# An encoder layer in 3-way split float32 on one core: gating two token tiles from SBUF, the prompt's weight remainders on VectorE, and three pairs of copies exchanged

## The chip, the core and the metric

The kernel runs on one core of a Trainium2 chip. Its engines are TensorE (PE in the profile, with PEld for its weight loads), VectorE (DVE), ScalarE (ACT), GpSimd (POOL) and SyncE (SP), which here issues nearly all DMAs. The metric is device time in microseconds (us). The kernel before takes 946.03 us, the median of three runs (943.36 to 946.63).

## The reference

One encoder layer is applied, with the same weights, to a prompt of 256 tokens and a sample of 2048 tokens of width 1024. What must be computed, cut to what matters here:

```python
h = rms_norm(x, g_pre)
q, k, v, z_a, u_f, z_f = split(h @ w_in)            # six parts of 512 columns
y_a = neighbourhood_attention(q, k, v, rpb)         # 64-column grid, 8x16 windows, 8 heads
y_f = fft2(u_f over tokens and 64 channels).real @ w_fourier + b_fourier
mixed = concat(rms_norm(y_a, g_na) * silu(z_a), rms_norm(y_f, g_f) * silu(z_f))
out = x + rms_norm(mixed @ w_out, g_post)
```

All is float32. The factors g_na and g_f are folded into the weights of `w_out`, and the inverse norm of a token is applied after that product, so the product's input from the Fourier half is `y_f * silu(z_f)`: this is the gating that the change moves.

## The kernel before

A float32 product is made of three matmuls: each operand is split into a rounded high part (a cast to float32r) and the remainder (operand minus high part), and `mm3` (L171) adds high·high, low·high and high·low. So before each product one engine casts (most often ACT) and one subtracts (most often DVE).

The program runs in stages. TensorE's order is written out throughout. In the first stages, up to `man.close()` at L961, the order of the other engines is written out too: they run in the order of the code. After that a scheduler orders ACT, DVE, POOL and SP, until the last quarter of the Fourier output (L1342), from where the order is the code's again.

- **Projections v and u of the first six token tiles** (L601 to L742). `x_split(c)` casts tile c (L293, ACT) and takes its remainder (L296, DVE). `diag` (L327, ACT) spreads the tokens' inverse norms over ten 128x128 diagonals, `dg`, which `spread` (L321) transposes on TensorE into PSUM. `r_sum` (L467, DVE) and `r_put` make sums of weights and store them.
- **The prompt's other four projections** (L745 to L783): sixteen steps b, each with 24 matmuls of 256 columns. `b_raw(b + 2)` casts the weights of step b + 2 (L578, ACT) and takes the remainder `wl` (L579), on GpSimd for the four weights in `WP` and on VectorE for the others. Between them VectorE scales and sums the sample's input for the next stage (L417, L440, L446), and `op_split` (L495) prepares that stage's first weights.
- **The sample's projections** (L785 to L959), Fourier stages (L961 to L1073).
- **Fourier output** (L1310 to L1365): four blocks e of 128 channels. `y_mm` makes three pieces ti of a block on TensorE, `y_out` adds the bias (L1264, ACT) and combines them into `Y` (L1272, DVE), a block's 2304 tokens. Tokens 0 to 255, the first two tiles of 128, come from piece ti = 2. `Y` is stored to DRAM (`yD`), its squares are summed by ACT and POOL (L1332 to L1340). The first tile needs all four blocks: its three first blocks are read back from `yD` together with the gate `zD` (L1317, L1318), multiplied on POOL (L1320), the fourth on DVE (L1349), cast to `y0h` (L1351), and its remainder is taken (L1353). The second tile is read back whole (L1357, L1358) and multiplied on POOL by `ys_mul` (L1409).
- **Attention with the Fourier half of the last product** (L1557 to L1673): 36 groups of (head pair, rows). Step k transposes the weights of group k - 2 (`transp`, L1479, into four PSUM tiles `ptb`, copied to SBUF half by ACT and half by DVE, L1492), makes the scores of group k (L1181), and multiplies group k - 2 with v (L1511). Even steps also make one token tile of the Fourier half (`f_mm`, L1442, matmuls at L1432), the first of which is `ftiles[0]` at L1562. Groups of the prompt (i = 0) and of two rows' ends (i = 1) have squares that ACT takes first (L1535, L1539).
- **The attention half of the last product, norm and output** (L1676 to L1773).

DMAs are issued by SP in the program's order; each also waits for the eighth DMA before it.

Of the kernel before, what the change touches and what calls it, by code (L numbers as in the profile page):

```python
# [25 lines left out]
NG = 13  # L26
NK = 16
BP = (3, 5)
WP = (7, 9, 11, 13)

HALF = ((0, 28), (4, 8), (12, 16), (20, 24))
KW = (24, 32, 32, 24)
# [144 lines left out]
def build(tc, A, O):  # L177
# [397 lines left out]
    def b_raw(b):  # L575
        wh, wl = [gt(BS, F32R, "w" + x) for x in "hl"]
        src = wp_[b]
        nc.scalar.copy(wh, src)  # L578
        (nc.gpsimd if b in WP else nc.vector).tensor_tensor(out=wl, in0=src, in1=wh.bitcast(F32), op=ALU.subtract)  # L579
        wb[b] = wh, wl  # L580


# [124 lines left out]
    for c in range(3, 6):  # L707
        if c < 5:
            wz_load(3)
        if c == 3:  # L710
            diag(0, 2)
            diag_group(0)
        if c < 5:
            x_split(c + 1)
        if c == 3:
            for q in range(8):
                r_sum(q)
        if c == 4:
            n_load((0, 0))
            for x in range(1, 5):  # L720
                r_put(x)
            xp = k8(F32, "xp", (128, KC, 256))
            hp_, lp_ = [k8(F32R, "p" + x, (128, KC, 256)) for x in "hl"]
            for k in range(KC):
                for t in range(2):
                    ts = slice(128 * t, 128 * t + 128)
                    nc.vector.scalar_tensor_tensor(out=xp[:, k, ts], in0=xs[t][:, k], scalar=gpre[:, k:k + 1],
                                                   in1=ivt[:, ts], op0=ALU.mult, op1=ALU.mult)
            nc.scalar.copy(hp_, xp)
            nc.vector.tensor_tensor(out=lp_, in0=xp, in1=f_(hp_), op=ALU.subtract)  # L730
        if c == 5:
            n_load((1, 0))
            b_raw(0)
            b_raw(1)
        p_mm("v", c, range(4))
        vu_out("v", c)
        p_mm("u", c, range(4))
        if c == 3:
            ivt = ps.tile([128, 256], F32, tag="c", name="ivt", bufs=1)
            spread(ivt, 0, 2)  # L740
            spread_group(0)
        vu_out("u", c)  # L742
# [493 lines left out]
    pg = ExitStack()  # L1236
    sm = pg.enter_context(tc.tile_pool(name="smY", bufs=2))
    sqy = pq_.enter_context(tc.tile_pool(name="sqy", bufs=1, side="right"))
    y0 = sqy.tile([128, 2, 4, 128], F32, name="y0")
    for t, (g, x) in enumerate(zip(G, (0, 512))):  # L1240
        g["w"] = []
        for w in g["kw"]:
# [19 lines left out]
    def y_out(e, ti, p1, p2, n, f=None):  # L1262
        t1 = sm.tile([128, 386], F32, tag="t1", name="t1", bufs=3)
        nc.scalar.activation(t1[:, :n], p1[:, :n], AF.Identity, bias=bfs[:, e:e + 1])  # L1264
        if f:
            f()

        def comb(out, sl, op, view=None):
            a, b = t1[:, sl], p2[:, sl]
            if view is not None:  # L1270
                a, b = view(a), view(b)
            nc.vector.tensor_tensor(out=out, in0=a, in1=b, op=op)  # L1272

        nk = 4 if ti == 2 else 6
        k20 = 6 * ti
        v3 = lambda a: a.rearrange("p (k l) -> p k l", l=64)
        l0 = 1 if ti else 0
        Y3 = Y[:, TP:].rearrange("p (k l) -> p k l", l=128)
        comb(Y3[:, k20:k20 + nk, l0:64], slice(0, nk * 64), ALU.subtract, lambda a: v3(a)[:, :, l0:64])
        kend = 15 - k20 - nk  # L1280
        comb(Y3[:, 15 - k20:kend if kend >= 0 else None:-1, 127:64:-1], slice(0, nk * 64), ALU.add,
             lambda a: v3(a)[:, :, 1:64])
        Yt = Y[:, TP:].rearrange("p (k l) -> p k l", l=64)
        col = lambda a: a.rearrange("p (k l) -> p k l", l=64)[:, :, 0:1]
        if ti == 0:
            comb(Yt[:, 30:20:-2, 0:1], slice(64, 384), ALU.add, col)
        elif ti == 1:
            comb(Yt[:, 12:16:2, 0:1], slice(0, 128), ALU.subtract, col)
            comb(Yt[:, 20:16:-2, 0:1], slice(0, 128), ALU.add, col)
            comb(Yt[:, 1:9:2, 0:1], slice(128, 384), ALU.subtract, col)  # L1290
            comb(Yt[:, 31:23:-2, 0:1], slice(128, 384), ALU.add, col)
        else:
            comb(Yt[:, 9:17:2, 0:1], slice(0, 256), ALU.subtract, col)
            comb(Yt[:, 23:15:-2, 0:1], slice(0, 256), ALU.add, col)
            comb(Y[:, TP + 1024:TP + 1025], slice(256, 257), ALU.subtract)
            comb(Y[:, 0:129], slice(257, 386), ALU.subtract)
            comb(Y[:, 255:128:-1], slice(258, 385), ALU.add)
            nc.sync.dma_start(yD[1, e, :, :TP], Y[:, :TP])

    def first_soft(g, f=None):  # L1300
        if f:
# [9 lines left out]
    for e in range(4):  # L1311
        Y = sqy.tile([128, T], F32, tag="Y", name="Y", bufs=3)
        if e < 3:
            for ti in (2, 0, 1):
                y_out(e, ti, *y_mm(e, ti))
                if e == 2 and ti == 2:
                    nc.sync.dma_start(y0[:, 0, :3], yD[1, :3, :, :128].rearrange("c p t -> p c t"))  # L1317
                    nc.sync.dma_start(y0[:, 1], zD[0, :, :128].rearrange("(c p) t -> p c t", p=128))  # L1318
                if e == 2 and ti == 0:
                    nc.gpsimd.tensor_tensor(out=y0[:, 0, :3], in0=y0[:, 0, :3], in1=y0[:, 1, :3], op=ALU.mult)  # L1320
            nc.sync.dma_start(yD[1, e, :, TP:], Y[:, TP:])
            if e == 0:
                load_wo1(1)
# [5 lines left out]
            for i in range(T // SQ if e < 2 else 1):  # L1329
# [7 lines left out]
                else:  # L1337
# [8 lines left out]
        py = y_mm(e, 0)  # L1346
        y0h = gt([128, 2, 4, 128], F32R, "y0h")
        y0h = [y0h[:, 0], y0h[:, 1]]
        nc.vector.tensor_tensor(out=y0[:, 0, 3], in0=Y[:, :128], in1=y0[:, 1, 3], op=ALU.mult)  # L1349
        sq = sm.tile([128, SQ], F32, tag="sqf", name="sqf", bufs=2)  # L1350
        y_out(e, 0, *py, lambda: (nc.scalar.copy(y0h[0], y0[:, 0]),  # L1351
                                  nc.scalar.activation(sq[:, :TP], Y[:, :TP], AF.Square)))
        nc.vector.tensor_tensor(out=y0h[1], in0=y0[:, 0], in1=y0h[0].bitcast(F32), op=ALU.subtract)  # L1353
        soft(G[0], 0)
        soft(G[0], 1)

        nc.sync.dma_start(y0[:, 0], yD[1, :, :, 128:256].rearrange("c p t -> p c t"))  # L1357
        nc.sync.dma_start(y0[:, 1], zD[0, :, 128:256].rearrange("(c p) t -> p c t", p=128))  # L1358
        scores(G[1])
        py = y_mm(e, 1)  # L1360
        first_soft(G[1])
# [114 lines left out]
        n = len(ds)  # L1476
        rsq_ops(inva[:, ds[0]["i"]:ds[0]["i"] + n], p[:, :n], n, 1.0 / 512)

    def transp(g):  # L1479
        g["pt"] = []  # L1480
        for b, ch in enumerate(g["ch"]):
            m = len(ch)
# [5 lines left out]
                        ys, x = slice(64 * y, 64 * y + 64), 64 * (h * m + j)  # L1488
                        nc.tensor.transpose(ptb[2 * b + y][:nk, x:x + 64], g["w"][b][ys, h, c0:c0 + nk], ident[ys, ys])  # L1489
            ov = o.rearrange("p h (j y x) -> p y h j x", y=2, x=64)  # L1490
            for y, copy in ((0, nc.scalar.copy), (1, V.tensor_copy)):
                copy(ov[:z, y, :, :m], ptb[2 * b + y][:z, :128 * m].rearrange("p (h j x) -> p h j x", h=2, x=64))  # L1492
            g["pt"].append(o)

# [61 lines left out]
           6: [(Y2, 1664, 2304), (Y, 1110, 1708)], 8: [(Y, 1708, 2304)]}  # L1556
    ftiles[0]["h"], ftiles[0]["l"] = y0h  # L1557
    y_parts(ftiles[1])
    ftiles[1]["raw"], ftiles[1]["z"] = y0[:, 0], y0[:, 1]
    for x in (slice(TP, TP + 512), slice(TP + 512, T)):  # L1560
        nc.sync.dma_start(yD[1, 3, :, x], Y[:, x])
    f_mm(ftiles[0], 0)  # L1562
    f_norm(range(2))
    ys_mul(ftiles[1])
    ptb += [ps.tile([128, 512], F32, tag="b", name="ptb", bufs=2) for x in range(2)]
    for x in range(2, 4):
        V.memset(ptb[x], 0.0)
# [9 lines left out]
    for k in range(2, len(G) + 2):  # L1577
# [15 lines left out]
            y = k - 24  # L1593
            nc.sync.dma_start(WO[y % 2][:, y // 2].bitcast(F32), woD[0, y % 2, y // 2])
        x = k // 2
        if k % 2 and g and i < 2:
            run_squares()
        transp(f)
        run_squares()
        if k % 2:  # L1600
            if g:
# [188 lines left out]
```

## Time and profile before

| | |
|---|---|
| median of three runs | 946.03 us |
| profiled execution | 947.1 us, of which the span is 945.3 us |
| PE busy | 929.2 us (98%) |
| DVE busy | 670.4 us (71%) |
| ACT busy | 470.3 us (50%) |
| POOL busy | 343.7 us (36%) |
| DMA | 265.02 MB, mean 280 GB/s |
| mean granted clock | 0.995 |

The span runs from the first to the last instruction of the profiled execution; 1.8 us of its time lie outside. A busy time counts an engine's own work. Where TensorE is busy nearly all the time, what counts is the little time in which it is idle or clocked down, and which engine or transfer ended that.

### The profile page before, as it was taken

The page shows a single profiled execution, that of the slowest core. Times are in us where ns is not written, and L with a number is a line of the kernel's source. Part 1 is how long each engine was busy: PE and PEld are TensorE (multiplying, and loading weights), DVE is VectorE, ACT ScalarE, POOL GpSimd, SP SyncE. Part 2 cuts the span into 40 slices and gives each one's busy share as a digit, 9 for nine tenths or more (in the row PEclk, how much of TensorE's full clock was granted, in tenths as well). Part 3 has the DMA queues.
Part 4 walks back from the last instruction along what each step waited for, and adds up shares of the span by engine and source line. Part 5 has one row for each costly group of instructions (what it writes and reads, how often), then busy time and mean ns, then how long its engine had stood idle before and what let it go on. Part 6 is the DMA issues. An engine that isn't in the chain of part 4 may idle for free.

```text
span 945.3 us, 18908 instructions
## 1 busy us (share of the span) xinstructions
PE 929.2 (98%) x6790; PEld 777.4 (82%) x6790; DVE 670.4 (71%) x1304; ACT 470.3 (50%) x1038; POOL 343.7 (36%) x340
## 2 busy tenths in 40 slices
PE   9999999999999999999999999899999999999996
PEld 7879988888888888888888898778787887888885
DVE  5468998687864977597666545568666665659997
ACT  5747577633232643233344326457556666654443
POOL 2201302436650300363343100445456565424444
PEclk9999999999999999999999999999999999999999
DMA  8899767468573999759979788779788899869993
GB/s 307 324 354 386 242 230 299 154 247 312 205 288 151 357 396 354 275 188 324 326 275 312 256 312 280 284 232 274 243 243 271 267 288 284 268 228 373 339 344 125
DMA packets 146861, 265.02 MB, mean 280 GB/s; under 512 B 21896, under 2 KB 86664, under 8 KB 144016
## 3 DMA queue, kind: packets, MB, share of 16 engines
q1 hardware_dynamic: 146608, 263.79, 80.5%
q8 instruction: 54, 0.88, 0.4%
q14 instruction: 39, 0.32, 0.1%
q10 hardware_dynamic: 160, 0.02, 0.0%
HBM read 175.21 MB, written 95.88 MB: 287 GB/s over the span
## 4 chain that ended last, share of the span: by engine, by line
PE 83%; DMA 3%; DVE 1%; issue 1%; ACT 0%; POOL 0%; DVEq 0%; SPq 0%; ACTq 0%
PE mm L173 15%; PE mm L174 15%; PE mm L172 15%; PE ptb L1432 11%; PE po L1432 10%; PE pv L1511 5%; PE ptb L1489 3%; PE s L1181 2%; PE pab L1007 2%; PE ptb L1181 2%; DMA yD<-Y 1%; DMA wo<-woD 1%; DMA vr<-wv 0%; DMA y<-yD 0%; PE pz L174 0%
## 5 line engine op out<-in xcount | busy, mean ns | idle before, releaser
L172 PE MATMUL mm<-xh,wa 128*128 128x512 f32 x448 | 174.4, 389 | 0.0
L174 PE MATMUL mm<-xh,wa 128*128 128x512 f32 x448 | 174.3, 389 | 0.0
L173 PE MATMUL mm<-xl,wa 128*128 128x512 f32 x448 | 174.3, 389 | 0.0
L172 PEld LDWEIGHTS mm<-xh,wa 128*128 128x128 f32 x448 | 84.1, 188 | 17.5
L174 PEld LDWEIGHTS mm<-xh,wa 128*128 128x128 f32 x448 | 84.1, 188 | 17.4
L173 PEld LDWEIGHTS mm<-xl,wa 128*128 128x128 f32 x448 | 84.1, 188 | 17.4
L1432 PE MATMUL ptb<-wo,yh 128*128 128x512 f32 x272 | 86.8, 400 | 0.0
L1432 PE MATMUL po<-w,yh 128*128 128x512 f32 x280 | 86.8, 391 | 0.0
L1215 POOL TENSOR_SCALAR w<-w,m 128x352 f32<-128x352 f32 (+4 forms) x136 | 75.3, 573 | 30.7 <-PE s L1181 14.2
L549 POOL TENSOR_TENSOR ws<-wr 128x512 f32<-128x512 f32 x16 | 21.4, 1338 | 176.8 <-DMA wr<-wz 160.1
L564 DVE TENSOR_TENSOR wa<-wr,wa 128x512 fp32r<-128x512 f32 x60 | 59.9, 1005 | 31.2 <-ACT wa L563 31.2
L1208 ACT ACTIVATE w<-w,m 128x352 f32<-128x352 f32 (+4 forms) x136 | 69.9, 521 | 13.2 <-DVE m L1203 12.9
L863 DVE TENSOR_TENSOR f<-u,mm 128x512 f32<-128x512 f32 x64 | 43.6, 681 | 35.1 <-PE mm L174 30.4
L173 PE MATMUL mm<-vl,xh 128*128 128x512 f32 x168 | 65.6, 390 | 0.2 <-DVE vl L495 0.2
L174 PE MATMUL mm<-vh,xl 128*128 128x512 f32 x168 | 65.4, 389 | 0.0
L172 PE MATMUL mm<-vh,xh 128*128 128x512 f32 x168 | 65.4, 389 | 0.0
L1432 PEld LDWEIGHTS ptb<-wo,yh 128*128 128x128 f32 x272 | 49.3, 188 | 14.8 <-ACT sqa L1539 3.1
L1432 PEld LDWEIGHTS po<-w,yh 128*128 128x128 f32 x280 | 52.3, 188 | 11.0
L563 ACT CAST wa<-wr 128x512 fp32r<-128x512 f32 x60 | 36.6, 617 | 45.5 <-PE mm L174 22.1
L1511 PEld LDWEIGHTS pv<-pt,v 96*64 96x64 f32 (+2 forms) x1280 | 45.2, 137 | 11.6 <-issue 6.6
L1432 PE MATMUL po<-w,yl 128*128 128x512 f32 x140 | 54.5, 389 | 0.0
L1432 PE MATMUL ptb<-wo,yl 128*128 128x512 f32 x136 | 53.1, 390 | 0.0
(252 smaller groups left out, 2208.1 us busy)
## 6 DMA issues: line engine op xcount, KB each, us to landing
wr<-wz SPq DMA_DIRECT2D x48, 512.0 KB
vl<-sD SPq DMA_DIRECT2D x20, 512.0 KB
xm<-xm SPq DMA_DIRECT2D x9, 1024.0 KB
oD<-ofs SPq DMA_DIRECT2D x18, 512.0 KB
of<-oD SPq DMA_DIRECT2D x18, 512.0 KB
yr<-yD SPq DMA_DIRECT2D x34, 256.0 KB
zD<-f SPq DMA_DIRECT2D x16, 512.0 KB
woD<-wo SPq DMA_DIRECT2D x16, 512.0 KB
```

The costliest lines, as they stand in the source:

```text
L172: nc.tensor.matmul(out, lh, rh, start=first, stop=False)
L173: nc.tensor.matmul(out, lh, rl, start=False, stop=False)
L174: nc.tensor.matmul(out, ll, rh, start=False, stop=last)
L563: nc.scalar.copy(o[:, 0], src)
L564: nc.vector.tensor_tensor(out=o[:, 1], in0=src, in1=o[:, 0].bitcast(F32), op=ALU.subtract)
L863: nc.vector.tensor_tensor(out=dst(f, b), in0=src(uu[u]), in1=src(p), op=op)
L1181: nc.tensor.matmul(sp[2 * b + h][64 * y:64 * y + 64, j * w:(j + n) * w], g["q"][hs, 128 * b + 64 * y:128 * b + 64 * y + 64], kk[hs, k:k + ...
L1208: nc.scalar.activation(w, w, AF.Exp, bias=m[:, h:h + 1], scale=-1.0, accum_out=m[:, 2 + h:3 + h])
L1215: nc.gpsimd.tensor_scalar(w, w, m[:, 4 + h:5 + h], 1.0, ALU.mult, ALU.mult)
L1432: nc.tensor.matmul(p, (d["l"] if x == 2 else d["h"])[:, c], w(n, int(x == 1), c), start=j == 0, stop=j == 11)
L1489: nc.tensor.transpose(ptb[2 * b + y][:nk, x:x + 64], g["w"][b][ys, h, c0:c0 + nk], ident[ys, ys])
L1511: nc.tensor.matmul(p[hs, b, o], v[:nk, b, x, hs], g["pt"][b][:nk, h, j * 128 + o.start:j * 128 + o.stop], start=first, stop=last)
```

## The change

Four edits, and nothing else:

1. `WP` is gone: the four remainders of the prompt's weights that GpSimd took are taken by VectorE, in the same places of the code.
2. At c = 3 of the first stage `x_split(4)` stands ahead of the two `diag` calls, no longer behind them.
3. `y0` holds 256 tokens instead of 128. Its gate half is loaded once, before the Fourier output. Each block's first 256 tokens are multiplied straight from `Y`, on GpSimd for blocks 0 to 2 and on VectorE for block 3. The store of these tokens to `yD` and both read-backs are gone, and so are `ys_mul` of tile 1 and its gate load.
4. In `transp` a switch exchanges the two engines of the copies: in steps 9, 19 and 27 (odd k, i below 2) VectorE copies y = 0 and ScalarE y = 1.

```diff
-WP = (7, 9, 11, 13)
...
-        (nc.gpsimd if b in WP else nc.vector).tensor_tensor(out=wl, in0=src, in1=wh.bitcast(F32), op=ALU.subtract)
+        nc.vector.tensor_tensor(out=wl, in0=src, in1=wh.bitcast(F32), op=ALU.subtract)
...
         if c < 5:
             wz_load(3)
+        if c < 5:
+            x_split(c + 1)
         if c == 3:
             diag(0, 2)
             diag_group(0)
-        if c < 5:
-            x_split(c + 1)
-        if c == 3:
             for q in range(8):
                 r_sum(q)
...
-    y0 = sqy.tile([128, 2, 4, 128], F32, name="y0")
+    y0 = sqy.tile([128, 2, 4, TP], F32, name="y0")
+    nc.sync.dma_start(y0[:, 1], zD[0, :, :TP].rearrange("(c p) t -> p c t", p=128))
...
-            nc.sync.dma_start(yD[1, e, :, :TP], Y[:, :TP])
...
-                if e == 2 and ti == 2:
-                    nc.sync.dma_start(y0[:, 0, :3], yD[1, :3, :, :128].rearrange("c p t -> p c t"))
-                    nc.sync.dma_start(y0[:, 1], zD[0, :, :128].rearrange("(c p) t -> p c t", p=128))
-                if e == 2 and ti == 0:
-                    nc.gpsimd.tensor_tensor(out=y0[:, 0, :3], in0=y0[:, 0, :3], in1=y0[:, 1, :3], op=ALU.mult)
+                if ti == 2:
+                    nc.gpsimd.tensor_tensor(out=y0[:, 0, e], in0=Y[:, :TP], in1=y0[:, 1, e], op=ALU.mult)
...
-        nc.vector.tensor_tensor(out=y0[:, 0, 3], in0=Y[:, :128], in1=y0[:, 1, 3], op=ALU.mult)
+        nc.vector.tensor_tensor(out=y0[:, 0, 3], in0=Y[:, :TP], in1=y0[:, 1, 3], op=ALU.mult)
...
-        y_out(e, 0, *py, lambda: (nc.scalar.copy(y0h[0], y0[:, 0]),
+        y_out(e, 0, *py, lambda: (nc.scalar.copy(y0h[0], y0[:, 0, :, :128]),
...
-        nc.vector.tensor_tensor(out=y0h[1], in0=y0[:, 0], in1=y0h[0].bitcast(F32), op=ALU.subtract)
+        nc.vector.tensor_tensor(out=y0h[1], in0=y0[:, 0, :, :128], in1=y0h[0].bitcast(F32), op=ALU.subtract)
...
-        nc.sync.dma_start(y0[:, 0], yD[1, :, :, 128:256].rearrange("c p t -> p c t"))
-        nc.sync.dma_start(y0[:, 1], zD[0, :, 128:256].rearrange("(c p) t -> p c t", p=128))
...
-    def transp(g):
+    def transp(g, swap=False):
...
-            for y, copy in ((0, nc.scalar.copy), (1, V.tensor_copy)):
+            for y in range(2):
+                copy = V.tensor_copy if swap != (y > 0) else nc.scalar.copy
...
-    ftiles[1]["raw"], ftiles[1]["z"] = y0[:, 0], y0[:, 1]
+    ftiles[1]["raw"] = y0[:, 0, :, 128:]
...
-    ys_mul(ftiles[1])
...
-        if k % 2 and g and i < 2:
+        first = bool(k % 2 and g and i < 2)
+        if first:
             run_squares()
-        transp(f)
+        transp(f, first)
```

How the instructions stand now, at the places where they move. TensorE's own order is the same in both.

VectorE in steps b = 8 to 12 of the prompt's projections (`wl` is a weight remainder, `nx` and `nt` are the sample's input and its sums), before:

```order
L579 TENSOR_TENSOR wl<-wr,wh 128x1024
L440 TENSOR_TENSOR nt<-nx 128x2048
L440 TENSOR_TENSOR nx<-nx 128x2048
L579 TENSOR_TENSOR wl<-wr,wh 128x1024
L440 TENSOR_TENSOR nx<-nt,nx 128x2048
L440 TENSOR_TENSOR nx<-nx 128x2048
L579 TENSOR_TENSOR wl<-wr,wh 128x1024
```

and in the change, where lines of code have numbers one lower:

```order
L578 TENSOR_TENSOR wl<-wr,wh 128x1024
L439 TENSOR_TENSOR nt<-nx 128x2048
L578 TENSOR_TENSOR wl<-wr,wh 128x1024
L439 TENSOR_TENSOR nx<-nx 128x2048
L578 TENSOR_TENSOR wl<-wr,wh 128x1024
L439 TENSOR_TENSOR nx<-nt,nx 128x2048
L578 TENSOR_TENSOR wl<-wr,wh 128x1024
L439 TENSOR_TENSOR nx<-nx 128x2048
L578 TENSOR_TENSOR wl<-wr,wh 128x1024
```

Two remainders come in among the sums; the other two stand in the same way between the scalings (L417) of steps 5 and 7. On GpSimd four rows `wl<-wr,wh` are gone from this stage.

ScalarE at c = 3 of the first stage (`dg` are the diagonals, `xh` the high part of tile 4), before:

```order
L351 ACTIVATE uo<-mm,invt 128x512 x3
L327 ACTIVATE dg<-onesq,invt 128x128 x10
L293 CAST xh<-xr 128x1024
L351 ACTIVATE vo<-mm,invt 128x512
```

and in the change:

```order
L350 ACTIVATE uo<-mm,invt 128x512 x3
L292 CAST xh<-xr 128x1024
L326 ACTIVATE dg<-onesq,invt 128x128 x10
L350 ACTIVATE vo<-mm,invt 128x512
```

The cast has moved ahead of the ten diagonals.

SP around the Fourier output (`y_5173` is `y0`), before:

```order
L1119 DMA q<-qD 128x2x128
L1298 DMA yD<-Y 128x256
L1321 DMA yD<-Y 128x2048
L1298 DMA yD<-Y 128x256
L1318 DMA y_5173<-zD 128x4x128
L1321 DMA yD<-Y 128x2048
L1317 DMA y_5173<-yD 128x3x128
L1298 DMA yD<-Y 128x256
L1357 DMA y_5173<-yD 128x4x128
L1358 DMA y_5173<-zD 128x4x128
L1561 DMA yD<-Y 128x512
```

and in the change:

```order
L1117 DMA q<-qD 128x2x128
L1316 DMA yD<-Y 128x2048 x2
L1555 DMA yD<-Y 128x512
```

Seven DMAs of this stretch are gone and one more ahead of it; the single load `y_5173<-zD 128x4x256` now stands nine DMAs ahead of that `q`, directly behind the loads of `za`.

GpSimd in the same stage (`sqs` is the sum of squares), before:

```order
L1340 TENSOR_TENSOR sqs<-sqs,sqf 128x288 x8
L1336 TENSOR_TENSOR sqs<-sqs,sqf 128x256
L1320 TENSOR_TENSOR y_5173<-y_5173 128x384
L1215 TENSOR_SCALAR sc<-sc,m_5174 128x128 x2
```

and in the change:

```order
L1335 TENSOR_TENSOR sqs<-sqs,sqf 128x288
L1315 TENSOR_TENSOR y_5173<-Y,y_5173 128x256 x2
L1335 TENSOR_TENSOR sqs<-sqs,sqf 128x288 x5
L1315 TENSOR_TENSOR y_5173<-Y,y_5173 128x256
L1335 TENSOR_TENSOR sqs<-sqs,sqf 128x288 x2
L1331 TENSOR_TENSOR sqs<-sqs,sqf 128x256
L1213 TENSOR_SCALAR sc<-sc,m_5175 128x128 x2
```

The scheduler has put the multiplications of blocks 0 and 1 behind the first addition of squares and that of block 2 behind the sixth.

## The prediction

> **What bounds the kernel now.** First the page: its first part gives each engine's busy time.
>
> ```profile
> PE 929.2 (98%) x6790; PEld 777.4 (82%) x6790; DVE 670.4 (71%) x1304; ACT 470.3 (50%) x1038; POOL 343.7 (36%) x340
> ```
>
> TensorE is idle for 945.3 - 929.2 = 16.1 us in all, so I asked next for TensorE's waits, longest in total first (total, times, longest).
>
> ```profile
> PE ptb L1432 <- issue: 4.1, 1, 4.1
> PE mm L174 <- DVE wl L579: 1.5, 2, 1.3
> ...
> PE mm L174 <- DVE xl L296: 0.5, 1, 0.5
> ```
>
> Three of the edits aim at these rows; the fourth aims at a wait of 0.16 us. The longest, 4.1 us, has no named releaser; the chain of waits between 585 and 625 us names it (start, us, what).
>
> ```profile
> 596.65 8.90 DMA yD<-Y
> 605.63 3.69 DMA y<-yD
> 609.39 1.00 POOL y L1320
> 610.41 0.62 ACT y0h L1351
> ...
> 612.53 5.40 PE ptb L1432 x12
> ```
>
> Tokens go to DRAM, come back, are multiplied and cast, and only then does TensorE start `f_mm(ftiles[0], 0)`. The windows of 1 us (busy, granted clock, DMA share, GB/s) show a second cost.
>
> ```profile
> 611.00:612.00 1.00, 0.00 (x0) 0.50 0.00 0
> ...
> 616.00:617.00 1.00, 1.00 (x4) 0.50 0.28 102
> 617.00:618.00 1.00, 1.00 (x6) 0.64 1.11 442
> ```
>
> The clock falls to 0.50 during the stop and stays there for five more us of matmuls. Undisturbed, the same twelve matmuls take 2.95 us in the same chain of waits, asked over the whole span:
>
> ```profile
> 633.72 2.95 PE ptb L1432 x12
> ```
>
> So this place costs 4.1 us of stop and 5.40 - 2.95 = 2.45 us of slow clock.
>
> **Edit 3, the gate from SBUF.** The store, both read-backs and the wait for them go. What sets the start of `f_mm` then? The last block's multiplication, cast and remainder. VectorE, ScalarE and GpSimd in that stretch (start, duration, idle before):
>
> ```profile
> 603.28 1.33 DVE L1272 TENSOR_TENSOR Y<-t,py 128x252 f32<-128x252 f32 x7
> 606.38 0.29 DVE L1349 TENSOR_TENSOR y<-Y,y 128x128 f32<-128x128 f32 x1 [1.77 <-DMA y<-zD]
> 606.60 1.08 DVE L1272 TENSOR_TENSOR Y<-t,py 128x384 f32<-128x384 f32 x3
> 611.06 0.69 DVE L1353 TENSOR_TENSOR y0h<-y,y0h 128x512 fp32r<-128x512 f32 x1 [3.39 <-ACT y0h L1351]
> ```
>
> ```profile
> 595.06 5.39 POOL L1340 TENSOR_TENSOR sqs<-sqs,sqf 128x288 f32<-128x288 f32 x7 [2.52 <-ACT sqf L1339]
> 600.42 0.73 POOL L1336 TENSOR_TENSOR sqs<-sqs,sqf 128x256 f32<-128x256 f32 x1
> ```
>
> `Y` of the last block is there at 603.28 + 1.33 = 604.6; 256 columns of two SBUF inputs take some 0.42 us on VectorE (twice 128 at 0.29, less the fixed part), the cast 0.62, the three combinations 1.08 beside it, the remainder 0.69: about 605.7 for the high part and 606.7 for the remainder. GpSimd's new third multiplication (0.73 by the row of the same 256 columns) stands among the additions of squares and pushes the last two, and with them ScalarE's squares and bias copies, by up to 0.7 us; then it is 606.4 and 607.4. TensorE gets there here:
>
> ```profile
> 608.05 0.34 PE L174 MATMUL py<-abh,pql 128*128 128x384 f32 x1
> 612.53 5.40 PE L1432 MATMUL ptb<-wo,y0h 128*128 128x512 f32 x12 [4.14 <-issue]
> ```
>
> That is at 608.4, a good us later, so the stop goes whole and the clock has no reason to fall: -4.1 - 2.45 = -6.55, say **-6.6 us**. The bounds: nothing less than -4.1 if the clock dips all the same, nothing more than -6.6. [...]
>
> What is hidden: the first two multiplications on GpSimd lie in its idle 2.52 us ahead of 595.06. They need the gate load, 512 KB that SP issues behind `za`, so at 581.83 + 1.42 = 583.25, some nine us ahead of that idle stretch:
>
> ```profile
> 581.83 1.42 SPq L1159 DMA_DIRECT2D za<-zD  x2
> ```
>
>  A 256 KB load of the same kind landed 3.69 us after its issue (the chain above). Behind the new start nothing fixed in time waits: the prompt's scores and tile 1's data are earlier too, and the next load that depends on `Y` (tile 2) is needed over ten us later.
>
> **Edits 1 and 2, the first stages.** They act on one chain, so they go together. VectorE around the prompt's steps:
>
> ```profile
> 78.87 1.23 DVE L579 TENSOR_TENSOR wl<-wr,wh 128x1024 fp32r<-128x1024 f32 x1 [3.81 <-ACT wh L578]
> ...
> 101.95 2.28 DVE L440 TENSOR_TENSOR nt<-nx 128x2048 f32<-128x2048 f32 x1
> 104.27 4.38 DVE L440 TENSOR_TENSOR nx<-nx 128x2048 f32<-128x2048 f32 x1
> ...
> 109.71 4.50 DVE L440 TENSOR_TENSOR nx<-nt,nx 128x2048 f32<-128x2048 f32 x1
> ...
> 117.59 2.28 DVE L446 TENSOR_TENSOR xl<-nx,xh 128x2048 fp32r<-128x2048 f32 x1
> 119.79 1.22 DVE L579 TENSOR_TENSOR wl<-wr,wh 128x1024 fp32r<-128x1024 f32 x1
> ```
>
> It never pauses from 78.87 on, and TensorE's 1.5 us are for its last two remainders. So four more of 1.22 us on VectorE should cost TensorE 4 x 1.14 (neighbours overlap by 0.08: 117.59 + 2.28 - 119.79) = +4.56 us. But two of the sums take 4.38 and 4.50 us where equal ones take 2.28, and these two coincide with GpSimd's remainders:
>
> ```profile
> 103.23 3.27 POOL L579 TENSOR_TENSOR wl<-wr,wh 128x1024 fp32r<-128x1024 f32 x1 [2.71 <-ACT wh L578]
> 108.99 3.07 POOL L579 TENSOR_TENSOR wl<-wr,wh 128x1024 fp32r<-128x1024 f32 x1 [2.49 <-ACT wh L578]
> ```
>
> The stretch, 4.38 - 2.28 = 2.10 and 4.50 - 2.28 = 2.22, is about the overlap (104.27 to 106.50, and 109.71 to 112.06). With GpSimd idle it goes: -4.32. Net for VectorE's last remainder: **+0.2 us** (bounds +4.56 if the stretch has another cause, and 0).
>
> Edit 2 removes this wait:
>
> ```profile
> 54.23 0.50 PE L174 MATMUL mm<-wc,xl 128*128 128x512 f32 x1 [0.53 <-DVE xl L296]
> ```
>
> ScalarE ahead of it:
>
> ```profile
> 48.95 3.02 ACT L327 ACTIVATE dg<-onesq,invt 128x128 f32<-128x128 f32 x10
> 51.88 1.03 ACT L293 CAST xh<-xr 128x1024 fp32r<-128x1024 f32 x1
> ```
>
> The ten diagonals take 3.02 us ahead of the cast; behind it they end about 0.95 us later (its 1.03, less the overlap), at 52.9, where the last of the transposes would like them at about 52.7, so 0.2 to 0.3 of the 0.53 comes back as a wait there. TensorE is some 0.3 us ahead, but VectorE decides the end of the prompt's steps, so that is swallowed at 120, unless VectorE's busy stretch starts earlier as well. VectorE's sums of weights do start 1.8 us earlier. Yet its stretch begins with a cast that stands behind this row on ScalarE:
>
> ```profile
> 77.22 0.69 ACT L351 ACTIVATE uo<-mm,invt 128x512 f32<-128x512 f32 x1 [3.11 <-DMA vN<-vo]
> ```
>
> A store issued at 71 us has to land, and the DMA engines are full then (share 1.01):
>
> ```profile
> 60.00:80.00 20.00, 20.00 (x107) 17.28 (x106) 14.22 (x24) 8.31 (x9) 0.00 (x0) 1.00 1.01 398
> ```
>
> Issued earlier, it stands behind the same bytes. I take no gain there (bounds 0 and -1.3, until TensorE's own result at about 75.9 would be waited for). Edits 1 and 2 together: **+0.1 us**, from -1.2 to +4.6.
>
> **Edit 4, the copies.** In step 27 ScalarE takes squares first, then copies the first `ptb` tile, for which the scores wait:
>
> ```profile
> 778.82 1.02 DVE L1492 COPY pt<-ptb 96x384 f32<-96x384 f32 x2
> 779.13 0.85 ACT L1492 COPY pt<-ptb 96x384 f32<-96x384 f32 x2
> 779.65 0.32 PE L1181 MATMUL ptb<-kk,q 64*64 64x128 f32 x1 [0.16 <-ACT pt L1492]
> ```
>
> VectorE's copies start at 778.82, ScalarE's at 779.13: 0.31 us. In steps 9 and 19 the difference is about the same. At most 0.3 each, at least nothing where the product with v then waits for ScalarE's second copy: **-0.5 us**, between -0.9 and 0.
>
> **Sum.** Against the profiled execution, 947.1 us (span 945.3): -6.6 + 0.1 - 0.5 = -7.0, so 940.1. It lies 1.1 above the median of the runs shown (946.03; 943.36 to 946.63), so as a median of runs I forecast 946.0 - 7.0 = **939.0 us**, -0.74%.
>
> **Rivals.**
>
> *A, more: the first stages start earlier.* If the store at 71 us lands 1.2 us earlier, VectorE's stretch and TensorE's end of it move by as much: 937.8. For it: VectorE's and ScalarE's work ahead of it is 1.8 us earlier. Against: the DMA share of 1.01.
>
> *B, less: the remainders are not paid back.* Were the 4.38 and 4.50 us caused by something else, TensorE would pay 4.5 us at 117 to 121: 943.4. For it: the first and second remainder on GpSimd (91.7 and 97.5) stretched nothing that ran beside them. Against it: the stretch equals the overlap twice.
>
> *C, part of the stop stays.* Something that is early now is just late, 1 to 3 us ahead of `f_mm`: without a slow clock 940 to 942.
>
> *D, slower: the gate load holds GpSimd's queue.* The multiplication of block 0 stands behind the first addition (592.5), and behind it wait the other additions, ScalarE's next squares (two buffers), its bias copies behind those, VectorE's combinations, and TensorE's PSUM. TensorE stops once GpSimd is more than 1.2 us late (a combination frees a tile at 598.38 + 1.09 = 599.5 that is needed at 600.7).
>
> ```profile
> 598.38 1.09 DVE L1272 TENSOR_TENSOR Y<-t,py 128x384 f32<-128x384 f32 x3 [1.89 <-ACT t L1264]
> 600.67 0.34 PE L172 MATMUL py<-abh,pqh 128*128 128x386 f32 x1
> ```
>
> From a lateness of 1.2 + 7.0 - 2.45 = 5.8 us, which is with the slow clock, the kernel is slower than before, and 8 us late gives 939.0 + 6.8 + 2.45 = 948.3. Against it: the load must then take over 15 us from its issue; the longest in the chain of that stretch is 8.90.
>
> *E, the exchange does nothing* because the other engine's copy takes its place: 939.5, within the forecast's own range.
>
> **How the numbers follow.** Forecast with E 0.62 (own range 937 to 941), A 0.17, B 0.11, C 0.06, D 0.04. This kernel's measurements tell about 0.5%, 4.7 us, from no change, so the border is 941.3. Faster: nearly all of the forecast and A, some of C: 0.81. Same: B, most of C and a tail of the forecast: 0.15. Slower: 0.04. The range goes from A's lower end, with runs that differ by 0.3%, to short of B: 936.0 to 942.5.
>
> **What would show it.** Right: no wait of TensorE at the first L1432 row and clock 1.00 through 600 to 620; L440 rows of 2.28 throughout; TensorE's waits for `wl` spread over steps 11 to 15, their end where it was. Wrong: a wait for `y0h` or a PSUM tile between 592 and 612, GpSimd idle there for `y<-zD`, L440 still at 4.4, or a wait behind the first Fourier tile that is not in the rows above.

## The result, and the profile after

The change takes 939.58 us (median of 4 runs, 938.95 to 940.26) where the kernel before takes 946.33 (4 runs): a ratio of 0.9935, with a 95% interval from 0.9912 to 0.9958. The forecast was 939.0. The profiled execution is one of 940.26 us with a span of 938.4. Three executions of the runs below, of 1038.72, 5234.43 and 5255.48 us, were in a slow state, and the medians given here are those of the others.

TensorE's waits in the profile after, longest in total first (total, times, longest); start-up rows left out:

```profile
PE mm L173 <- DVE wl L578: 1.6, 4, 1.0
...
PE py L1258 <- DVE w L1062: 0.8, 1, 0.8
...
PE ptb L1482 <- DVE m L1201: 0.4, 1, 0.4
...
PE ptb L1482 <- DVE ofs L1456: 0.3, 1, 0.3
```

The row of 4.1 us is gone, and so is the row for `xl`. The waits for `wl` are four now, no longer two, with nearly the same sum. Two rows are new: 0.8 us for `w`, at 580 us, and 0.4 us for `m`, a per-row value of the softmax, at 676 us.

The chain of waits between 585 and 625 us has the first Fourier tile directly behind the last matmul, and the windows of 1 us keep the clock (behind the five engines' busy times stands the clock, then the DMA share and GB/s):

```profile
608.16 0.18 PE py L173
608.34 2.76 PE ptb L1425 x12
```

```profile
607.00:608.00 1.00, 1.00 (x8) 1.00 (x7) 1.00 (x9) 0.85 (x4) 1.00 (x3) 1.00 0.00 0
609.00:610.00 1.00, 1.00 (x6) 0.82 (x5) 0.38 (x1) 0.59 (x3) 0.46 (x2) 1.00 0.07 16
611.00:612.00 1.00, 1.00 (x8) 0.90 (x7) 0.09 (x1) 0.36 (x2) 0.00 (x0) 1.00 0.31 115
```

TensorE is fully busy and at full clock where it stood still and then ran at 0.50. What feeds it, on VectorE:

```profile
604.70 0.43 DVE L1344 TENSOR_TENSOR y<-Y,y 128x256 f32<-128x256 f32 x1
...
606.03 0.68 DVE L1348 TENSOR_TENSOR y0h<-y,y0h 128x512 fp32r<-128x512 f32 x1
...
607.03 0.35 DVE L1201 CUSTOM_DVE_ANT_1 sc<-ptb,tb 128x192 f32<-128x192 f32 x1
```

The remainder of `y0h` is done at 606.71. The third row is the first scores' softmax, which reads the PSUM tile `ptb` that the Fourier tile is then written to; it ends at 607.38. TensorE arrives at 608.18. So the two things that the tile needs are ready 1.5 and 0.8 us ahead of it.

In the first stages, the start of VectorE's busy stretch, the two of its four sums that took 4.38 and 4.50 us before, and the first work behind its last remainder:

```profile
78.13 1.23 DVE L578 TENSOR_TENSOR wl<-wr,wh 128x1024 fp32r<-128x1024 f32 x1 [6.68 <-ACT wh L577]
...
106.79 2.30 DVE L439 TENSOR_TENSOR nx<-nx 128x2048 f32<-128x2048 f32 x1
...
110.13 2.30 DVE L439 TENSOR_TENSOR nx<-nt,nx 128x2048 f32<-128x2048 f32 x1
...
122.34 4.64 DVE L494 TENSOR_TENSOR vl<-vr,vh 128x1024 fp32r<-128x1024 f32 x4
```

All four sums take 2.30 us; none is stretched. From 78.13 to 122.34 is 44.21 us with four more remainders; before, from 78.87 to 123.13, it was 44.26.

Where the time went is seen by taking the start of one and the same matmul in both traces (TensorE's order is equal). The lead of the change over the kernel before:

| TensorE's position (matmuls counted from 0) | before, us | lead of the change, us |
|---|---|---|
| 200th matmul, ahead of every edit | 49.54 | 1.80 |
| 720th matmul, behind the prompt's projections | 128.85 | 0.78 |
| 2900th matmul | 578.29 | 0.96 |
| last matmul of the Fourier output | 608.05 | 0.05 |
| last matmul | 937.74 | 7.02 |

The first 1.80 us are no work of the change: both programs are the same up to there. They are used up on the way to 608, and then 6.8 us come at the one place. Behind it the lead goes from 6.83 us to 7.02: of what edit 4 brings, the new wait for `m` takes 0.4 back.

### The profile page after: what moved, and what is told of

It is laid out like the page before. It is cut to its first block, busy times and chain, and to the rows that moved or that the text cites. A ratio compares the mean times of both kernels' runs of the same rounds, so it can differ in the third digit from the quotient of the medians.

```text
span 938.4 us, 18894 instructions
## 1 busy us (share of the span) xinstructions
PE 925.6 (99%) x6790; PEld 774.4 (83%) x6790; DVE 671.1 (72%) x1308; ACT 469.3 (50%) x1038; POOL 331.9 (35%) x337
```

## The experiments

**Edit 3 alone.** The first run does what the change does to `y0`, `yD` and the gate load, and nothing else.

```diff
-    y0 = sqy.tile([128, 2, 4, 128], F32, name="y0")
+    y0 = sqy.tile([128, 2, 4, TP], F32, name="y0")
+    nc.sync.dma_start(y0[:, 1], zD[0, :, :TP].rearrange("(c p) t -> p c t", p=128))
...
+                if ti == 2:
+                    nc.gpsimd.tensor_tensor(out=y0[:, 0, e], in0=Y[:, :TP], in1=y0[:, 1, e], op=ALU.mult)
...
-    ys_mul(ftiles[1])
```

> Only edit 3 (the gate from SBUF), the rest as before. My theory: the whole 4.1 us stop ahead of the first Fourier tile and the 2.45 us of half clock go, so the time is 6.5 us under before (about 939.6) and TensorE's start of that tile, seen against the matmul ahead of it, is 4.1 us earlier. Rival C (part of the stop stays, about 2 us of it): 4 us under before. Rival 'it came from edits 1, 2 and 4': under 2 us.

Measured: 940.05 us against 945.66, ratio 0.9943 (0.9926 to 0.996), so 5.6 us under before. In its trace the tile follows the last matmul without a stop and takes 2.92 us for the twelve:

```profile
606.63 0.34 PE L174 MATMUL py<-abh,pql 128*128 128x384 f32 x1
606.81 2.92 PE L1427 MATMUL ptb<-wo,y0h 128*128 128x512 f32 x12
```

The gain is edit 3's, at the low side of what was expected. The interval, 3.8 to 7.0 us, holds the expected 6.5 too; the clock, further below, gives a reason for less.

**Edit 1 alone.**

```diff
-        (nc.gpsimd if b in WP else nc.vector).tensor_tensor(out=wl, in0=src, in1=wh.bitcast(F32), op=ALU.subtract)
+        nc.vector.tensor_tensor(out=wl, in0=src, in1=wh.bitcast(F32), op=ALU.subtract)
```

> Only edit 1 (all remainders of the prompt's weights on VectorE). Theory (the two stretched sums were stretched by GpSimd's remainders): the two L440 rows of 4.38 and 4.50 us fall to 2.3, VectorE's last remainder of that stage ends within 0.4 us of where it was, time against before +0.2 us. Rival B (the sums are slow for another cause): L440 stays at 4.4 in two rows, VectorE's end is 4.5 us later, time +4.5 us.

Measured: 945.85 against 945.66, ratio 1.0005 (0.9994 to 1.0016). The two sums on VectorE, and the bounds of its stretch:

```profile
78.04 1.23 DVE L578 TENSOR_TENSOR wl<-wr,wh 128x1024 fp32r<-128x1024 f32 x1 [3.90 <-ACT wh L577]
...
106.72 2.28 DVE L439 TENSOR_TENSOR nx<-nx 128x2048 f32<-128x2048 f32 x1
...
110.06 2.28 DVE L439 TENSOR_TENSOR nx<-nt,nx 128x2048 f32<-128x2048 f32 x1
...
122.27 2.35 DVE L494 TENSOR_TENSOR vl<-vr,vh 128x1024 fp32r<-128x1024 f32 x2
```

4.38 and 4.50 us have become 2.28, the stretch is 44.23 us long. With the stretch of these two sums gone, the four remainders are paid back, and rival B falls: its +4.5 us would be 1.0048, well outside the interval.

**Edit 2 alone.**

```diff
+        if c < 5:
+            x_split(c + 1)
         if c == 3:
             diag(0, 2)
             diag_group(0)
-        if c < 5:
-            x_split(c + 1)
-        if c == 3:
```

> Only edit 2 (the cast of token tile 4 ahead of the ten diagonals). Theory: the 0.53 us wait for xl goes and 0.2 to 0.7 us come back as a wait of the transposes for the diagonals; VectorE's sums of weights start 1.8 us or more earlier; the store that ScalarE waits for at 77 us lands at the same time, since the DMA engines are full there, so VectorE's busy stretch starts at 78.9 as before and the time is within 0.3 us of before. Rival A: that store lands 1.2 us earlier, VectorE's busy stretch starts at 77.7, time -1.2 us.

Measured: 946.14 against 945.66, ratio 1.0006 (0.9996 to 1.0016): no change, as the theory has it. VectorE's stretch began at 76.95 here, earlier than rival A asks for. But it began at 77.28 with edit 3 alone and at 78.04 with edit 1 alone, where the cast stands as before. The start of that stretch differs by almost two microseconds between executions, whatever stands on ScalarE, so rival A is not shown, and the time gives nothing for it. Its one trace can't settle it either: TensorE waited 1.8 us for `wl` there, and the clock was at half from 116.77 to 120.18 us, which by an estimate cost it up to 1.7 us (half of 3.41).

**Edit 4 alone.**

```diff
-            for y, copy in ((0, nc.scalar.copy), (1, V.tensor_copy)):
+            for y in range(2):
+                copy = V.tensor_copy if swap != (y > 0) else nc.scalar.copy
```

> Only edit 4 (the copies of steps 9, 19 and 27 exchanged). Theory of the prediction: the 0.16 us wait for pt in step 27 goes, and in each of the three steps TensorE is up to 0.3 us earlier behind it: together -0.5 us on TensorE, too little for the time itself to tell (945.2 against 945.7). Rival E: the product with v waits instead for the other engine's copy, nothing is gained in TensorE's position over the three steps.

Measured: 945.18 against 946.19, ratio 0.9989 (0.9977 to 1.0002). By TensorE's position against before there are three steps and next to nothing between them: 0.19 us at 669 us, 0.22 at 731, 0.25 at 780, together 0.66. The row for `pt` has gone from the waits. Rival E falls; the time alone would not tell it.

**Filling the stop.** To price the slow clock apart from the stop, sixteen matmuls without use were put into the stop of the kernel before; first into the Fourier tile's own PSUM tile, then, as below, into one of their own.

```diff
+    fill = ps.tile([128, 512], F32, tag="c", name="pfill", bufs=1)
+    for j in range(16):
+        nc.tensor.matmul(fill, wo1[0][0][:, 0, :128], wo1[0][0][:, 0], start=True, stop=True)
     f_mm(ftiles[0], 0)
```

> Before, with sixteen more matmuls of 128x512 on TensorE ahead of the first Fourier tile (their result is written over at once), about 3.7 us of work that fills the 4.1 us stop. The round trip through DRAM stays. If the half clock comes from the stop (theory), the first twelve matmuls of the tile take 2.9 instead of 5.4 us, the tile starts where it did, and the time is 2.45 us under before (943.6). If the clock falls for another cause, the twelve still take 5.4 us and the time is that of before.

> Before, with sixteen more matmuls of 128x512 (3.7 us at full clock) ahead of the first Fourier tile, this time into a PSUM tile of their own, so that they need not wait for the tile that the softmax of the first scores still reads. Theory: TensorE stays busy over most of the stop, the clock stays at 1.00, the first twelve matmuls of the tile take 2.9 us instead of 5.4, the tile starts where it did (12 rows later than the last matmul of the Fourier output by 4.1 us), and the time is 1 to 2.5 us under before, by whether the clock of before is low for one or two of its 3.4 us stretches. Rival (the clock falls for another cause than the stop): 5.4 us again, time as before.

Both missed: 951.40 (1.006, 1.0039 to 1.0081) and 949.89 (1.0041, 1.0023 to 1.0058), slower than before. The fillers did not fill the stop, they stood behind it. TensorE of the first and of the second:

```profile
611.28 5.50 PE L1563 MATMUL ptb<-wo 128*128 128x512 f32 x16 [4.11 <-DVE m L1203]
```

```profile
610.51 6.37 PE L1564 MATMUL pfill<-wo 128*128 128x512 f32 x16 [3.89 <-DVE m L1203]
```

They need nothing of `y0`, and yet waited 4.11 and 3.89 us, for the softmax on VectorE. VectorE of the second:

```profile
609.37 0.69 DVE L1353 TENSOR_TENSOR y0h<-y,y0h 128x512 fp32r<-128x512 f32 x1 [3.39 <-ACT y0h L1351]
...
610.11 0.34 DVE L1203 CUSTOM_DVE_ANT_1 sc<-s,tb 128x192 f32<-128x192 f32 x1
```

The softmax reads the scores out of PSUM, and in VectorE's queue it stands behind the remainder of `y0h`, which waits for the round trip through DRAM. The first PSUM tile comes free at 610.11 + 0.34 = 610.45, and TensorE goes on at 610.51. So the round trip held TensorE in two ways: `y0h` itself was missing, and the queue behind it kept the PSUM tiles. In the kernel before, the remainder ended at 611.06 + 0.69 = 611.75, and TensorE began only at 612.53:

```profile
612.07 0.35 DVE L1203 CUSTOM_DVE_ANT_1 sc<-ptb,tb 128x192 f32<-128x192 f32 x1
```

This row, 0.7 us behind the remainder, is what the page called "issue". The chain that the prediction quoted goes from the cast of `y0h` straight to TensorE; between them stand the remainder and this softmax. What the fillers were meant for, a price for the clock alone, they did not give; the other runs do.

**Which remainders cost VectorE something.** In the kernel before, the two remainders on GpSimd that lay beside scalings (L417) stretched nothing (2.72 us for four, both times), and the two beside sums (L440) did (4.38 and 4.50 us for 2.28). Two kernels take the change and put back one pair each.

```diff
+WP = (7, 9)
...
-        nc.vector.tensor_tensor(out=wl, in0=src, in1=wh.bitcast(F32), op=ALU.subtract)
+        (nc.gpsimd if b in WP else nc.vector).tensor_tensor(out=wl, in0=src, in1=wh.bitcast(F32), op=ALU.subtract)
```

> The change, with two of the four remainders (b = 7 and 9) back on GpSimd, where VectorE has only scalings (scalar_tensor_tensor, L416) beside them. Theory (a tensor_tensor of GpSimd and one of VectorE on SBUF exclude each other, a scaling excludes nothing): GpSimd's rows take 2.27 us plus what is left of the tensor_tensor that VectorE is in when they start; the scalings stay at 0.66 each; VectorE's last remainder of the stage ends 2.3 us earlier than in the change against the start of its busy stretch (44.2 us from 78.13 to 122.34 become 41.9), and TensorE's waits for wl (1.6 us) nearly go. Rival (GpSimd slows whatever VectorE does beside it): the four scalings beside each remainder stretch by 2 us in all, VectorE's stretch stays at 44 us. In time: -1 to -1.6 us against the change by the theory, 0 by the rival; the time alone cannot tell this.

Measured: 936.59 against 946.19, ratio 0.9897 (0.9872 to 0.9922). GpSimd, then VectorE beside it:

```profile
88.97 2.73 POOL L579 TENSOR_TENSOR wl<-wr,wh 128x1024 fp32r<-128x1024 f32 x1 [61.01 <-ACT wh L578]
94.78 2.88 POOL L579 TENSOR_TENSOR wl<-wr,wh 128x1024 fp32r<-128x1024 f32 x1 [3.07 <-ACT wh L578]
```

```profile
88.20 1.22 DVE L579 TENSOR_TENSOR wl<-wr,wh 128x1024 fp32r<-128x1024 f32 x1
89.33 2.71 DVE L417 SCALAR_TENSOR_TENSOR nx<-nx,gpre,iv 128x512 f32<-128x512 f32 x4
...
94.17 1.22 DVE L579 TENSOR_TENSOR wl<-wr,wh 128x1024 fp32r<-128x1024 f32 x1
95.30 2.71 DVE L417 SCALAR_TENSOR_TENSOR nx<-nx,gpre,iv 128x512 f32<-128x512 f32 x4
```

The four scalings take 2.71 us with GpSimd at work beside them. VectorE's remainder is still running for 88.20 + 1.22 - 88.97 = 0.45 us when GpSimd starts, and 2.73 - 0.45 = 2.28; the second time 2.88 - 0.61 = 2.27. VectorE's stretch is 41.96 us long (76.00 to 117.96) where 41.9 was expected, and no wait of TensorE for `wl` is left.

The other pair, with `WP = (11, 13)`:

> The change with the other two remainders, b = 11 and 13, back on GpSimd: these lie beside VectorE's sums (tensor_tensor, L439). Theory (two tensor_tensor on SBUF exclude each other): two of the sums take 4.3 to 4.5 us, VectorE's stretch up to the first op_split is 44.2 - 2.3 + 4.3 = 46.2 us, TensorE waits 2 us longer for wl, time +2 us against the change. Rival (it counts how many are on GpSimd, not which): 41.9 us as with the first two, and a time under the change.

Measured: 942.25 us, ratio to before 0.9966 (0.9953 to 0.9978), where the change on the same chip had 0.9932 (0.9916 to 0.9948): 3.4 us slower than the change, where 2 were expected. GpSimd and VectorE:

```profile
102.84 4.92 POOL L579 TENSOR_TENSOR wl<-wr,wh 128x1024 fp32r<-128x1024 f32 x1 [73.69 <-ACT wh L578]
108.92 3.22 POOL L579 TENSOR_TENSOR wl<-wr,wh 128x1024 fp32r<-128x1024 f32 x1 [1.16 <-ACT wh L578]
```

```profile
103.23 2.29 DVE L440 TENSOR_TENSOR nt<-nx 128x2048 f32<-128x2048 f32 x1
105.55 4.36 DVE L440 TENSOR_TENSOR nx<-nx 128x2048 f32<-128x2048 f32 x1
109.83 3.40 DVE L579 TENSOR_TENSOR wl<-wr,wh 128x1024 fp32r<-128x1024 f32 x1
```

Here the victims are one sum and one remainder, not two sums, and each can be read to a few hundredths. GpSimd's row of 4.92 us ends at 107.76; VectorE's sum that began at 105.55 ends 2.15 us after that. GpSimd's second row ends at 112.14; VectorE's remainder of 3.40 us ends 1.09 after that. What looks like a slow instruction is one that stands still until the other engine is through, and then takes nearly its usual time (2.15 of 2.28, 1.09 of 1.22). The stretch came to 46.47 us (46.2 expected), TensorE's waits for `wl` rose by 1.1 us over the change's 1.6, and 0.5 for a remainder on GpSimd came to them. The two profiled executions on this chip lie 2.2 us apart, so of the 3.4 between the medians 1.2 are not accounted for. TensorE's waits:

```profile
PE mm L174 <- DVE wl L579: 2.7, 2, 2.3
...
PE mm L174 <- POOL wl L579: 0.5, 1, 0.5
```

So in these rows a VectorE instruction with two inputs in SBUF and GpSimd's remainder, which has two as well, were done one after the other, in both directions: GpSimd waited 0.45 and 0.61 us for the end of VectorE's remainder in the run with b = 7 and 9, VectorE stood still for 2.08 us (4.36 - 2.28) and 2.18 (3.40 - 1.22) in this one. The scalings, which take their second tensor from PSUM (`iv`), ran on beside GpSimd: four in 2.71 us, where the change, with GpSimd idle, has them in pairs of 1.40. Whether they are spared for the PSUM tensor or as another kind of instruction, no run here separates.

**The late start of VectorE's stretch.** The stretch starts behind a cast on ScalarE, which stands behind the write-out of `u`, which waits for a store (3.11 us in the kernel before). This kernel takes the cast out of there.

```diff
+        if c == 5:
+            b_raw(2)
         vu_out("u", c)
...
-        if b < 14:
+        if 0 < b < 14:
             b_raw(b + 2)
```

> The change, with the cast and remainder of the prompt's third weight (b = 2) ahead of the write-out of u of tile 5, which ScalarE begins only when an earlier store has landed. Theory (VectorE's stretch of 44 us starts late because that cast stands behind the wait of ScalarE for a store): VectorE starts its stretch at about 71 instead of 78.1, or as soon as the loads of the sample's input allow, and TensorE's waits for wl (1.6 us in the change) go, time -1 to -1.6 us against the change. Rival (something else, the loads of nx, the next weights or ScalarE's later casts, holds VectorE as well): its stretch has pauses, the last remainder ends where it did, no gain.

Measured: 939.16 us, ratio to before 0.9926 (0.9898 to 0.9954), no faster than the change. VectorE:

```profile
71.73 1.40 DVE L416 SCALAR_TENSOR_TENSOR nx<-nx,gpre,iv 128x512 f32<-128x512 f32 x2
79.19 1.22 DVE L578 TENSOR_TENSOR wl<-wr,wh 128x1024 fp32r<-128x1024 f32 x1 [6.05 <-ACT wh L577]
```

The scalings do start at 71.73, so their loads were there. But the next cast stands behind the same store, and VectorE pauses 6.05 us for that one. The rival is right: the stop moved by one instruction.

**The change beside the better ones.** Three kernels on one chip, five rounds each: the change; the change with `WP = (7, 9)`; and the latter with more warm-up ahead of the first projection.

```diff
-    for i in range(9):
+    for i in range(12):
         nc.tensor.matmul(hot, onesq, onesq, start=True, stop=True)
```

> The change itself, once more, beside the next three on the same chip. 939.6 as before it, 0.7% under before.

> The change with the remainders of b = 7 and 9 on GpSimd, timed against the change on the same chip. Theory (those two lie beside scalings, which GpSimd does not disturb; TensorE's 1.6 us of waits for wl go, and what is earlier there stays earlier): 1.5 to 3 us under the change. Rival (the first measurement owed its 3 us to the other chip or to the start): within 1 us of the change.

> The same with twelve warm-up products in place of nine ahead of the first projection, so that TensorE is busy until about 5.0 to 6.3 us and not 4.6 to 5.2. Theory (the granted clock changes only at the ends of stretches of 3.41 us, and a stretch with much idle time in it is followed by one at half clock): the clock is up by 7 us in each execution and does not fall again, TensorE's 200th matmul stands at 47.6 to 48.3 us where it was anywhere from 47.7 to 49.8, time 0.3 to 1 us under the kernel with nine. Rival (the start is set by the loads alone): the same time.

Measured, against 945.74 before:

| kernel | median, us | lowest to highest | ratio to before |
|---|---|---|---|
| change | 938.87 | 937.7 to 941.19 (6 runs) | 0.9932 (0.9916 to 0.9948) |
| change, b = 7 and 9 on GpSimd | 937.62 | 937.2 to 937.7 (5 runs) | 0.9913 (0.99 to 0.9927) |
| the same, twelve warm-up products | 936.95 | 935.66 to 937.94 (6 runs) | 0.991 (0.9896 to 0.9924) |

The second is 1.25 us under the change here; none of its runs was slower than the fastest of the change. That is less than the 1.5 expected, more than the rival's 1, and less than half of what the first comparison gave. The third is another 0.7 us lower, with runs that overlap those of the second, so the warm-up is not shown by the times. In its one trace TensorE's 200th matmul stands at 47.93 us, in the expected place, but the second kernel has it at 48.09 with nine.

## Why the prediction was right, and where it was not

**The sum.** Forecast -7.0 us, measured -6.75 in the first comparison and -6.87 (945.74 - 938.87) in the last. Alone, the parts measure -5.61 (edit 3), +0.19 (edit 1), +0.48 (edit 2) and -1.01 (edit 4), each with 0.1 to 0.2% (1 to 2 us) of uncertainty to both sides; together -5.95, within these uncertainties of -6.8.

**Edit 3, forecast -6.6.** The mechanism is right: no stop, no slow clock, and nothing that takes their place. Between the two profiled executions the place gave 6.77 us (a lead of 0.05 before it, 6.82 behind it). The size of its second term was one execution's luck. The clock term of 2.45 us was read from an execution in which the clock was low for almost seven microseconds. With edit 1 alone, where the stop stays, it was low for half as long. Windows of 1 us of that run:

```profile
611.00:612.00 1.00, 0.51 (x1) 0.50 (x2) 1.00 (x9) 0.85 (x4) 0.73 (x3) 0.64 0.07 20
612.00:613.00 1.00, 1.00 (x4) 0.76 (x3) 0.49 (x4) 1.00 (x6) 1.00 (x3) 0.50 0.88 258
613.00:614.00 1.00, 1.00 (x4) 0.81 (x3) 0.37 (x1) 0.59 (x3) 0.73 (x2) 0.50 0.91 262
614.00:615.00 1.00, 1.00 (x4) 0.76 (x4) 0.90 (x6) 0.00 (x0) 0.00 (x0) 0.66 0.03 9
```

A mean of 0.64 is 0.72 us at half clock, 0.66 is 0.68: 3.4 us in all. With edit 4 alone the same count goes from 610.8 to 617.6:

```profile
610.00:611.00 1.00, 0.00 (x0) 0.00 (x0) 0.91 (x4) 0.37 (x2) 0.00 (x0) 0.90 0.00 0
611.00:612.00 1.00, 0.44 (x1) 0.47 (x2) 1.00 (x7) 0.79 (x3) 0.96 (x3) 0.50 0.06 15
...
617.00:618.00 1.00, 1.00 (x7) 0.96 (x6) 0.00 (x0) 0.25 (x1) 0.00 (x0) 0.69 0.99 369
```

The twelve matmuls take accordingly:

```profile
611.49 4.49 PE L1431 MATMUL ptb<-wo,y0h 128*128 128x512 f32 x12 [4.13 <-issue]
```

```profile
611.56 5.46 PE L1432 MATMUL ptb<-wo,y0h 128*128 128x512 f32 x12 [4.12 <-issue]
```

So the slow clock costs 4.49 - 2.92 = 1.6 us in the one case and 2.5 in the other. The edit is worth 5.7 or 6.6 us, by the execution. Its own measurement of 5.6 lies at the former, but its interval holds both. The prediction took this term from the one row of before; the runs show both lengths, so that the forecast for the whole came so close is in part luck.

Which of the two it is goes with where the stop lies. In the three kernels with one stretch of 3.41 us at half clock TensorE was at work again 0.17 us before that stretch began, or 0.22 and 0.60 us after; in the three with two stretches it was 0.77, 1.57 and 1.63 us after. Six traces show this, and no run varies it on purpose.

The step "GpSimd stands among the additions, then it is 606.4 and 607.4" came out at 606.71 for the remainder; the slack was 1.5 us. The load that the prediction took for one of 256 KB moved three blocks, 192 KB; nothing hung on it. The prediction did not see the second thing that had to be ready, the PSUM tile, which was the nearer one with 0.8 us.

**Edits 1 and 2, forecast +0.1.** VectorE's stretch went from 44.26 to 44.21 us, where the working had 4.56 - 4.32 = +0.24. Rival B, at 0.11, fell with edit 1 alone. What the prediction read as a stretch in proportion to the overlap is one engine that waits for the other, and from that follows what it missed: only two of the four remainders had cost anything. Edit 1 moved all four, gained 2.3 us with two of them (46.47 us with them on GpSimd, 44.21 in the change) and gave 2.3 back with the other two (41.96). That is also why one of TensorE's four waits for `wl`, the longest with 1.01 us, stands at 98.70 us, in step 8, where the prediction had them in steps 11 to 15.

The step on the diagonals was mis-sized. It had 0.2 to 0.3 us come back at the transposes; in the profiled execution they took 2.37 us against 1.04:

```profile
50.23 2.37 PE L320 MATMUL iv<-ident,dg 128*128 128x128 f32 x8
```

TensorE was 1.80 us early there, from the start, while ScalarE was only 0.7 earlier, held by a store. That part of the lead went for this reason: in the second profiled execution of the change, where TensorE was 0.33 us early, and with edit 2 alone the eight followed one another nearly as before, so the term is anything from nothing to 1.3 us. As forecast, VectorE decided the end of the stage, and what TensorE had in hand was swallowed.

**Edit 4, forecast -0.5.** 0.66 us by TensorE's position, in the three steps named, when it stands alone. In the change the wait for `m` at 676 us takes 0.4 of it, in both profiled executions. The other kernels, those with the change and two remainders on GpSimd among them, don't have it, and the profile doesn't name what VectorE waits for there; the cause stays open.

**Another wait that no part named.** In the profile after, TensorE lost the rest of its lead at 580 us, in the row of 0.8 us for `w`. ScalarE:

```profile
579.29 0.62 ACT L1061 CAST w<-wr 32x512 fp32r<-32x512 f32 x1 [1.29 <-DMA wr<-wt]
```

The cast waited 1.29 us for its load of `wt`, and TensorE, 0.96 us earlier than before, waited 0.8 us for what the cast feeds. The second execution of the change has no such wait (its lead of 1.1 us passes 580 unhurt), so it is no price of every execution.

**The rivals.** C (part of the stop stays) and D (the gate load holds GpSimd's queue) did not happen: GpSimd's first product stands at 592.45 directly behind the addition, with nothing waited for.

```profile
591.68 0.80 POOL L1335 TENSOR_TENSOR sqs<-sqs,sqf 128x288 f32<-128x288 f32 x1 [17.39 <-PE py L1258]
592.45 1.44 POOL L1315 TENSOR_TENSOR y<-Y,y 128x256 f32<-128x256 f32 x2
```

What D would cost was not tried. A could not be separated from the scatter of that store between executions.

## What to carry to other kernels

When a wait is traced back, follow it also through the queue of the engine that ends it: an instruction that waits for a transfer kept back everything behind it here, and that was the release of PSUM, which even work without any need of the data had to wait for (4.11 and 3.89 us). Before work is moved between VectorE and GpSimd, look which VectorE instruction lies beside each piece: a pair that both read two tensors from SBUF was done one after the other here (a sum of 2.28 us took 4.36, a remainder of 1.22 took 3.40), a piece beside scalings that take a tensor from PSUM cost VectorE nothing (four in 2.71 us, in pairs of 1.40 without it), so move piece by piece and not all at once. Before a term is read from one execution, align the same matmul in two traces; where they differ ahead of every edit, or a slow clock has another length, the term has a range.

## What the hardware showed beyond what was expected

The granted clock changes in steps: at the stop it was low for 3.41 us in three of the kernels that have the stop (edit 1 alone, edit 2 alone, the first fillers) and for 6.83, twice as much, in three others (before, edit 4 alone, the second fillers), with stops of 3.9 to 4.3 us in all. Within a trace the changes lie whole multiples of 3.4133 us apart, to within 0.01 us: 600.75, 6.83 and 324.27 us in the kernel before (176, 2 and 95 times), 928.42 us in the change (272 times). In the kernel before, the 3.41 us ahead of the fall at 610.90 held 2.51 us without a matmul and the next 3.41 held 1.63, and behind each the clock was low; the third held none, and behind it the clock was whole again. So the fall did not come at a fixed time behind TensorE's last matmul: it came 2.5 us after that matmul had ended at 608.39 in the kernel before, 3.4 us after with edit 4 alone, 3.7 with edit 2 alone and 3.9 with edit 1 alone; and in the first stages of edit 2 alone the clock fell behind a wait of 1.8 us.

The start differs in the same way. The second projection matmul in the kernel before and in the change:

```profile
6.83 0.80 PE L173 MATMUL mm<-wc,xh 128*128 128x512 f32 x1
```

```profile
6.23 0.51 PE L172 MATMUL mm<-wc,xh 128*128 128x512 f32 x1 [0.28 <-DVE wc L262]
```

The clock came up at 10.15 us in the one (the matmuls take 0.63 us up to there and 0.39 from 10.30 on) and at 3.91 in the other, with one and the same program up to there, and in the second TensorE is 1.80 us earlier at the 200th matmul. That is half of the 3.6 us by which the first four runs of the kernel before lie apart (943.36 to 946.97).

GpSimd can lose its turn: with b = 11 and 13 on it, its row starts at 102.84, while VectorE was in a remainder that ended at 103.31, and then VectorE's next sum, begun at 103.23, went first and took its usual 2.29 us.

```profile
102.09 1.22 DVE L579 TENSOR_TENSOR wl<-wr,wh 128x1024 fp32r<-128x1024 f32 x1
```

So the row of 4.92 us holds 2.7 us of waiting, which the profile counts as busy.
